# Attention scores of a hybrid encoder in unsplit float32, two heads at a time on the halves of the array's rows

## The chip, the cores and the metric

The kernel runs on one core of a Trainium2 chip. A core has a matrix engine (TensorE, PE in the profile; PEld are its weight loads), a vector engine (VectorE, DVE), a scalar engine (ScalarE, ACT), GpSimd (POOL), and SyncE (SP), which here only issues transfers. Each engine works through its own queue in order, and semaphores tie the queues together. The metric is the device time of one execution in microseconds: before the change, the median of three runs is 2033.01 us (2028.2 to 2036.88).

## The reference

Two encoder layers over 1024 tokens of width 1024, in float32. The part of a layer that matters here, with 8 query heads, 2 key/value heads and 4 memory heads of 64 dimensions:

```python
h = _rmsnorm(x, g_pre_mix[l])
zf, zq, zk, zv, zm = jnp.split(h @ w_in[l], splits, axis=-1)
q = _rope(zq.reshape(b, s, 8, 64), positions)
k = _rope(zk.reshape(b, s, 2, 64), positions)
v = zv.reshape(b, s, 2, 64)
# window attention: block of 128 queries against its own and the two neighbouring blocks of keys
scores = jnp.einsum('bnqhgd,bnjhd->bnhgqj', qb, kb) * 64 ** -0.5
probs = softmax(concat([where(valid, scores, NEG_INF), sink]))[..., :-1]
y_a = jnp.einsum('bnhgqj,bnjhd->bnqhgd', probs, vb)
# memory attention: every token against 256 memory rows
km, vm = jnp.split(_rmsnorm(mem, g_mem[l]) @ w_mem_kv[l], 2, axis=-1)
scores = jnp.einsum('bshd,bmhd->bhsm', zm, km) * 64 ** -0.5
y_m = jnp.einsum('bhsm,bmhd->bshd', softmax(scores), vm)
x = x + _rmsnorm(concat(rms(y_f), rms(y_a), rms(y_m)) @ w_out[l], g_post_mix[l])
```

`y_f` is a Fourier mixing of `zf`. A gated feed-forward network (FFN) of inner width 2816 follows, with its own norms.

## The kernel before

Tokens are handled in 8 tiles of 128. To multiply in float32 accuracy, the kernel mostly splits a value into a high part of type `float32r` (a rounded copy, made by ACT) and a low part (the rest, made by DVE or POOL), and adds three products hi*hi, hi*lo, lo*hi in PSUM (`Acc`, line 187). Such a product goes through the array once. A few products take plain `float32` operands: transposes, norms' sums, and the values of attention in part.

A layer runs these stages, each woven from two or three streams of units (`weave`): projection to k, v and z (`kvz`, tile kvp) with the Fourier products (yfp); projection to q (`q`, tile qp) with the memory attention; the window attention of key head 0 (`att_units(0)`) with the output product of the Fourier and memory groups (tile mo); the window attention of key head 1 (`att_units(1)`) with the output product of the window group and the norms (hTp); then the FFN.

A head has 64 dimensions, the array 128 rows. Before the change the kernel fills both halves of the rows with one head: for q and z the upper or lower half holds the high part and the other half the low part (`q_stacks`: ACT casts line 435, DVE subtractions line 438). The keys hold, in two arrays, the high part twice and the low part twice (`dup_stacks`: ACT lines 424 and 425, DVE lines 428 and 429). So a score tile is two products on the whole array, q's stack by the high keys and by the low keys, line 788 for window scores (tile sc, 384 columns, or 256 at the two ends) and line 901 for memory scores (tile ms, 256 columns). DVE adds the mask and takes the row maximum (line 789) or the maximum alone (line 903), ACT takes the exponential (lines 801 and 906), POOL divides by the sum (lines 812 and 912). PE transposes the probabilities (tile pT line 825, mpT line 922), and the values' product follows.

For key head 0 (`g == 0`) the transposed probabilities are split (ACT line 176, DVE line 177), and v stands as high and low part side by side, so that line 840 (tile av) runs two products of 512 columns on the whole array; `fold` adds the two halves of the outcome (ACT line 861, DVE line 863). For key head 1 and for the memory the probabilities are copied in float32 by ACT (lines 830 and 924), and two products go to the two halves of the array's *columns*, one head or pair of heads on each (av line 833, mav line 932).

PSUM has two buffers each under the tags sc, pT, av and pd; score tiles take sc. A scheduler of the framework fixes each engine's order of instructions ahead of the run by its own estimate of times, so the order isn't that of the program's text: products whose operands or buffer it deems late are moved behind others.

On-chip memory is handed out by hand in numbered slots of 256 float32 per partition (`at`), in an area of float32r, an area of float32, and separate tiles (`TURNED`, `reflex`, `turned`) which can change type; a separate tile is taken anew once all readers of its earlier content are done.

Of the kernel before, what the change touches and what calls it, by code (L numbers as in the profile page):

```python
# [11 lines left out]
F32 = mybir.dt.float32  # L12
# [7 lines left out]
P = 128  # L20
D = 1024
S = 1024
# [17 lines left out]
TURNED = {32: 8, 56: 8, 112: 8, 120: 4}  # L40
# [29 lines left out]
def tile_encoder(ctx: ExitStack, tc: tile.TileContext, T, C, out):  # L70
# [89 lines left out]
    mps, phs, yys = Ring(56, 58, 32, 34), run(16, 3, 4), run(104, 2, 4)  # L160
# [259 lines left out]
    def dup_stacks(dsts, src):  # L420

        for j, (kh, kl) in enumerate(dsts):
            r, o = slice(64 * j, 64 * j + 64), slice(64 - 64 * j, 128 - 64 * j)
            nc.scalar.copy(kh[r], src[r])
            nc.scalar.copy(kh[o], src[r])
        for j, (kh, kl) in enumerate(dsts):
            r, o = slice(64 * j, 64 * j + 64), slice(64 - 64 * j, 128 - 64 * j)
            nc.vector.tensor_tensor(out=kl[r], in0=src[r], in1=f32(kh[r]), op=ALU.subtract)
            nc.vector.tensor_tensor(out=kl[o], in0=src[r], in1=f32(kh[r]), op=ALU.subtract)

    def q_stacks(dsts, src):

        for j, dst in enumerate(dsts):
            r = slice(64 * j, 64 * j + 64)
            nc.scalar.copy(dst[r], src[r])
        for j, dst in enumerate(dsts):
            r, o = slice(64 * j, 64 * j + 64), slice(64 - 64 * j, 128 - 64 * j)
            nc.vector.tensor_tensor(out=dst[o], in0=src[r], in1=f32(dst[r]), op=ALU.subtract)


    class Memory:
# [62 lines left out]
        def load(self):  # L504
            raw = at(32, 2, NMEM)
            nc.sync.dma_start(raw, kvd[self.l, :, 0:512].rearrange("p (i c) -> p i c", i=2))
            self.v = at(6, 2, 4, HD)
            nc.sync.dma_start(self.v, kvd[self.l, :, 512:1024].rearrange("p (t h d) -> p t h d", t=2, h=4))
            km = shaped(reflex(F32R), (2, 2, 2, NMEM))
            self.km = [km[:, i] for i in range(2)]  # L510
            for ci in range(2):
                dup_stacks([(self.km[ci][:, j, 0], self.km[ci][:, j, 1]) for j in range(2)], raw[:, ci])


    class Mix:
# [193 lines left out]
        def kvz_load(self):  # L709

            self.wkvz = load_w512(self.win, FW + AW, self.g)
            self.vst, self.zst, self.kvr = {}, {}, {}

        def kvz(self, t):
            half, c = divmod(t, 4)
            if c == 0:
                self.vst[half] = at(96 + 4 * half, 4, 2, 2, HD, dt=F32R)
                z = at(104 + 8 * half, 2, 2, 512, dt=F32R)
# [848 lines left out]
```

## Time and profile before

| | |
|---|---|
| median of three runs | 2033.01 us |
| lowest, highest | 2028.2, 2036.88 us |
| profiled execution's own time | 2032.38 us |
| span of its instructions | 2030.4 us |
| mean granted TensorE clock | 0.994 of full speed |

The profile page shows the busy time of each engine, then the costliest groups of instructions, each with line, engine, operation, written and read tiles, count, busy time, mean duration in ns, and the idle time before it with the work that ended it. The chain of waits follows the work that ended last back from the end, step by step. The profile names a float32r operand in a PE row f32 as well; what tells them apart is the line. A plain float32 product leaves two records for each product, and so does its weight load. "128\*64" in a PE row is a product that uses half the array's columns.

The layer's stages lie at about 85 to 140 us (kvz and Fourier), 140 to 200 (q and memory), 200 to 290 (window attention, key head 0) and 290 to 372 (key head 1) in layer 0, and about 1070 to 1380 in layer 1.

### The profile page before, as it was taken

What the parts mean: (1) busy time and instruction counts of PE and PEld (TensorE: products, weight loads), DVE (VectorE), ACT (ScalarE), POOL (GpSimd) and SP (SyncE); (2) the same over time, 40 slices, a digit from 0 to 9 for tenths busy, and PEclk for the clock granted to TensorE, in tenths of its full rate; (3) what the DMA queues carried; (4) which work ended last, traced back from release to release, by engine and by line L of the source; (5) the groups of instructions that cost most, each with busy time, mean ns of one, the idle gap of its engine ahead of it and who ended that gap; (6) DMA issues with size and microseconds to landing.
All of it is one profiled execution on the core that took longest, in us unless ns stands there. A gap on an engine that the chain in (4) does not pass through costs nothing.

```text
span 2030.4 us, 28325 instructions
## 1 busy us (share of the span) xinstructions
PE 1984.7 (98%) x9587; PEld 1631.2 (80%) x9587; DVE 1492.6 (74%) x2346; ACT 1049.7 (52%) x2204; POOL 684.9 (34%) x811
## 2 busy tenths in 40 slices
PE   8999999999999999999999999999999999999998
PEld 7877878778888888887888778877788888887886
DVE  5566767897877776778876668679786776778766
ACT  6476877643333333554555768686333333346441
POOL 4344445224334333002423644451433433410011
PEclk9999999999999999999999999999999999999999
DMA  6110333434333324879831113244333323269973
GB/s 213 62 58 22 109 104 115 146 109 130 104 109 100 103 88 139 297 266 324 286 142 54 54 58 115 85 144 135 106 118 114 116 82 114 96 209 354 314 265 125
DMA packets 181889, 288.56 MB, mean 142 GB/s; under 512 B 15560, under 2 KB 81648, under 8 KB 181744
## 3 DMA queue, kind: packets, MB, share of 16 engines
q1 hardware_dynamic: 173680, 267.88, 39.7%
q10 hardware_dynamic: 8064, 18.88, 2.4%
q8 instruction: 75, 1.23, 0.2%
q14 instruction: 70, 0.57, 0.1%
HBM read 220.11 MB, written 66.58 MB: 141 GB/s over the span
## 4 chain that ended last, share of the span: by engine, by line
PE 86%; DVE 5%; DMA 3%; ACT 2%; issue 2%; POOL 1%; SPq 0%; DVEq 0%; POOLq 0%; ACTq 0%
PE fo L1330 17%; PE qc L1181 11%; PE qx L1181 11%; PE qy L1181 11%; PE mo L187 8%; PE qz L1181 5%; PE kvp L187 4%; PE qp L187 3%; PE zT L187 2%; PE sc L788 2%; PE pT L825 2%; PE av L833 1%; PE qa L1181 1%; PE mav L932 1%; PE av L840 1%
## 5 line engine op out<-in xcount | busy, mean ns | idle before, releaser
L1330 PE MATMUL fo<-arena_r 128*128 128x512 f32 x1512 | 354.2, 391 | 6.0 <-ACT big L1355 3.8
L1330 PEld LDWEIGHTS fo<-arena_r 128*128 128x128 f32 x1512 | 283.6, 188 | 65.6 <-ACT big L1355 4.6
L176 ACT CAST arena_r<-arena_f 128x512 fp32r<-128x512 f32 (+2 forms) x344 | 185.9, 571 | 179.5 <-DMA arena_f<-actd 66.6
L1181 PE MATMUL qc<-arena_r,flex 128*128 128x512 f32 x912 | 220.2, 390 | 0.0
L177 DVE TENSOR_TENSOR arena_r<-arena_f,arena_r 128x512 fp32r<-128x512 f32 x262 | 182.0, 727 | 46.9 <-ACT arena_r L176 39.0
L1171 ACT CAST flex<-arena_f 128x512 fp32r<-128x512 f32 x148 | 91.9, 621 | 235.0 <-PE qy L1181 73.3
L1181 PEld LDWEIGHTS qc<-arena_r,flex 128*128 128x128 f32 x912 | 171.2, 188 | 37.0
L1181 PE MATMUL qy<-arena_r,flex 128*128 128x512 f32 x576 | 139.9, 390 | 2.3 <-ACT flex L1171 2.3
L1171 ACT CAST arena_r<-arena_f 128x512 fp32r<-128x512 f32 x92 | 57.1, 621 | 159.1 <-DVE arena_f L1168 63.6
L1172 DVE TENSOR_TENSOR flex<-arena_f,flex 128x512 fp32r<-128x512 f32 x148 | 110.9, 750 | 28.4 <-ACT flex L1171 28.2
L1181 PEld LDWEIGHTS qy<-arena_r,flex 128*128 128x128 f32 x576 | 107.9, 188 | 25.3 <-ACT flex L1171 2.7
L1215 POOL TENSOR_TENSOR arena_f<-arena_f 128x512 f32<-128x512 f32 x36 | 47.3, 1315 | 237.5 <-ACT arena_f L1186 237.5
L1181 PE MATMUL qx<-arena_r 128*128 128x512 f32 x360 | 119.5, 389 | 0.0
L1181 PE MATMUL qy<-arena_r 128*128 128x512 f32 x480 | 116.7, 390 | 0.0
L1172 DVE TENSOR_TENSOR arena_r<-arena_f,arena_r 128x512 fp32r<-128x512 f32 x92 | 68.2, 742 | 63.2 <-ACT arena_r L1171 62.8
L1181 PE MATMUL qz<-arena_r,flex 128*128 128x512 f32 x320 | 106.8, 395 | 0.0
L1181 PEld LDWEIGHTS qy<-arena_r 128*128 128x128 f32 x480 | 90.3, 188 | 18.9 <-ACT arena_r L1171 0.2
L1168 DVE TENSOR_TENSOR arena_f<-arena_f 128x512 f32<-128x512 f32 x90 | 98.1, 1098 | 5.5 <-DMA arena_f<-in_w_ffn_in 3.9
L1222 POOL TENSOR_TENSOR arena_f<-arena_f 128x512 f32<-128x512 f32 x36 | 60.0, 1667 | 120.2 <-DVE arena_f L1221 120.2
L187 PE MATMUL mo<-big,arena_r 128*128 128x512 f32 x384 | 100.2, 399 | 0.3 <-ACT arena_f L1031 0.2
L1181 PE MATMUL qx<-flex,flex 128*128 128x512 f32 x304 | 100.1, 390 | 0.0
L1242 POOL TENSOR_TENSOR arena_f<-arena_f,flex 128x512 f32<-128x512 f32 x32 | 51.8, 1619 | 139.5 <-ACT flex L1233 83.7
(315 smaller groups left out, 4659.8 us busy)
## 6 DMA issues: line engine op xcount, KB each, us to landing
arena_f<-in_w_ffn_out SPq DMA_DIRECT2D x264, 256.0 KB, 4.7
actd<-arena_f SPq DMA_DIRECT2D x154, 256.0 KB, 2.5
arena_f<-actd SPq DMA_DIRECT2D x154, 256.0 KB, 4.4
arena_f<-in_w_ffn_in SPq DMA_DIRECT2D x46, 512.0 KB, 3.7
big<-in_w_ffn_in SPq DMA_DIRECT2D x40, 512.0 KB, 4.5
arena_f<-in_w_in SPq DMA_DIRECT2D x40, 256.0 KB, 2.9
arena_f<-in_x SPq DMA_DIRECT2D x16, 512.0 KB, 4.3
arena_f<-in_w_out SPq DMA_DIRECT2D x32, 256.0 KB, 2.7
```

Source lines behind the costliest of these rows:

```text
L176: nc.scalar.copy(hi, src)
L177: return (lo_eng or nc.vector).tensor_tensor(out=lo, in0=src, in1=f32(hi), op=ALU.subtract)
L187: mm(self.dst, a, b, start=self.i == 0, stop=self.i == self.n - 1)
L788: mm(pt, lhs, self.kst[g][i][:, k0 * P : k1 * P], start=i == 0, stop=i == 1)
L1168: nc.vector.tensor_tensor(out=s, in0=x, in1=y, op=op)
L1171: self.cast = nc.scalar.copy(w[:, 0], s)
L1172: nc.vector.tensor_tensor(out=w[:, 1], in0=s, in1=f32(w[:, 0]), op=ALU.subtract)
L1181: mm(pt, a, b, start=start and n == 0, stop=n == 11, skip_group_check=not start)
L1215: G(out=self.u2, in0=self.u2, in1=self.p1, op=ALU.add)
L1222: G(out=self.p5, in0=self.p1, in1=self.p5, op=ALU.add)
L1242: (G if i % 2 else V).tensor_tensor(out=a[i], in0=c, in1=g[i], op=ALU.mult)
L1330: mm(pt, ab[:, 0, x, sl], ab[:, 1, y], start=new and first and j == 0, stop=last and j == 2, skip_group_check=not new)
```

## The change

q, z and the keys stay plain float32 and are not split. A pair of heads lies on the two halves of the rows: the even head's 64 dimensions on rows 0 to 63, the odd head's on rows 64 to 127, as the transposes leave them; keys of a window key head are copied to both halves, memory keys are as loaded. Each head's score tile is now one float32 product of 64 rows by 128 columns of the array, and the two heads of a pair write two PSUM buffers. The memory attention goes by pairs of heads and half as many tokens at a time. The values of key head 0 are done as those of key head 1 were; every other copy of transposed probabilities there is DVE's. `dup_stacks`, `q_stacks`, `fold` and `values_32` go. More slots become separate tiles, and two operands of the FFN and one ring change places.

```diff
-TURNED = {32: 8, 56: 8, 112: 8, 120: 4}
+TURNED = {16: 8, 32: 8, 56: 8, 64: 8, 72: 8, 80: 8, 96: 8, 104: 8, 112: 8, 120: 4}
...
-    mps, phs, yys = Ring(56, 58, 32, 34), run(16, 3, 4), run(104, 2, 4)
+    mps, yys = Ring(56, 58, 34, 14), run(88, 2, 4)
...
         def load(self):
-            raw = at(32, 2, NMEM)
-            nc.sync.dma_start(raw, kvd[self.l, :, 0:512].rearrange("p (i c) -> p i c", i=2))
+            self.k = at(32, 2, NMEM)
+            nc.sync.dma_start(self.k, kvd[self.l, :, 0:512].rearrange("p (i c) -> p i c", i=2))
...
-            km = shaped(reflex(F32R), (2, 2, 2, NMEM))
-            self.km = [km[:, i] for i in range(2)]
-            for ci in range(2):
-                dup_stacks([(self.km[ci][:, j, 0], self.km[ci][:, j, 1]) for j in range(2)], raw[:, ci])
...
-            split(vst[:, :, 0, :], vst[:, :, 1, :], r[:, P : 2 * P].rearrange("p (g d) -> p g d", g=2), nc.gpsimd)
+            nc.gpsimd.tensor_copy(self.v32[:, :, t, :], r[:, P : 2 * P].rearrange("p (g d) -> p g d", g=2))
...
-            q_stacks([self.zst[half][j][:, :, c * P : c * P + P] for j in range(2)], zt)
+            nc.scalar.copy(self.zf[:, half, :, c * P : c * P + P], zt)
...
-                dup_stacks([(self.kst[g][0][:, sl], self.kst[g][1][:, sl]) for g in range(2)], ktf)
+                for g, copy in enumerate((nc.scalar.copy, nc.vector.tensor_copy)):
+                    for o in range(2):
+                        copy(self.kf[64 * o : 64 * o + 64, g, sl], ktf[64 * g : 64 * g + 64])
...
-            q_stacks([self.qst[half][j][:, :, c * P : c * P + P] for j in range(2)], qt)
+            nc.scalar.copy(self.qf[half][:, :, c * P : c * P + P], qt)
...
-            for h in range(4):
-                pt = ps([W], "sc", "sc")
-                lhs = self.qst[half][h % 2][:, 2 * g + h // 2, c * P : c * P + P]
-                for i in range(2):
-                    mm(pt, lhs, self.kst[g][i][:, k0 * P : k1 * P], start=i == 0, stop=i == 1)
-                nc.vector.tensor_tensor_reduce(
-                    out=es_[h // 2][:, h % 2, :W], in0=pt, in1=mask[:, m0 : m0 + W], op0=ALU.add, op1=ALU.max,
-                    scale=1.0, scalar=-3e38, accum_out=rmax[:, h : h + 1],
-                )
+            for hp in range(2):
+                pts = [ps([W], "sc", "sc") for _ in range(2)]
+                for s in range(2):
+                    r = slice(64 * s, 64 * s + 64)
+                    mm(pts[s], self.qf[half][r, 2 * g + hp, c * P : c * P + P], self.kf[r, g, k0 * P : k1 * P], start=True, stop=True)
+                for s in range(2):
+                    nc.vector.tensor_tensor_reduce(
+                        out=es_[hp][:, s, :W], in0=pts[s], in1=mask[:, m0 : m0 + W], op0=ALU.add, op1=ALU.max,
+                        scale=1.0, scalar=-3e38, accum_out=rmax[:, 2 * hp + s : 2 * hp + s + 1],
+                    )
...
-                pp = phs(2, 512, dt=F32R)
-                ph, pl = pp[:, 0], pp[:, 1]
-                split(ph, pl, pT.rearrange("p h q -> p (h q)"))
-                lhs = self.vst[(k0 + j) // 4][:, (k0 + j) % 4, g].rearrange("p a d -> p (a d)")
-                for i, p_ in enumerate((ph, pl)):
-                    mm(av, lhs, p_, start=j == 0 and i == 0, stop=j == nk - 1 and i == 1)
...
+                (nc.vector.tensor_copy if (self.pfi % 2 and not g) else nc.scalar.copy)(pf, pT.rearrange("p (k s) q -> p s k q", s=2))
+                for s in range(2):
+                    rhs = pf[:, s].rearrange("p k q -> p (k q)")
+                    mm(av[64 * s : 64 * s + 64, 0 : 2 * P], self.v32[:, g, k0 + j], rhs, start=j == 0, stop=j == nk - 1)
+            nc.scalar.copy(dst, av[:, 0 : 2 * P].rearrange("p (k q) -> p k q", k=2))
+
+        def att_begin(self, g):
+
+            pf = turned((16, 112)[g], 4, 2, 2, P)
+            self.pfs, self.pfi = [pf[:, i] for i in range(4)], 0
             if g:
...
+                v = at(4, NT, HD)
+                nc.gpsimd.tensor_copy(v, self.v32[:, 1])
+                self.v32 = v[:, None].to_broadcast([P, 2, NT, HD])
+                reflex(F32R, 16)
+                reflex(F32R, 96)
...
-        def mem_scores(self, h, half):
+        def mem_scores(self, half, pr, b):
...
+            pts = [ps([2, NMEM], "ms", "sc") for _ in range(2)]
+            for j in range(2):
+                c = 2 * b + j
+                for s in range(2):
+                    r = slice(64 * s, 64 * s + 64)
+                    mm(pts[s][:, j], self.zf[r, half, pr, c * P : c * P + P], self.mem.k[r, pr], start=True, stop=True)
...
-    HB = {1: (64, 72), 2: (80, 88), 5: (16, 24), 6: (96, None), 3: (0, 8), 7: (32, 40), 4: (104, None)}
+    HB = {1: (64, 104), 2: (80, 72), 5: (16, 24), 6: (96, None), 3: (0, 8), 7: (32, 40), 4: (88, None)}
...
+            if i == 5:
+                reflex(F32R, 64)
+                reflex(F32R, 104)
             if 5 <= i < 9:
                 hb.plain(0, i - 5)
...
-                reflex(F32R, 112)
+                for k in (72, 80, 112):
+                    reflex(F32R, k)
```

The orders that the scheduler makes are shown at three places of layer 0; a row has the line, the operation, the tile written and the tiles read, the shape, and xN where N in a row are alike. The number behind a tile's name tells one use of it from another. After the change, line 762 holds the window scores, 855 the memory scores, 800 and 875 the transposes of probabilities, 806 and 885 the values' products.

PE in the window attention of key head 0, third block and after, before the change: each sc tile's two products stand together.

```order
L788 MATMUL sc_2281<-arena_r 128x384 x2
L788 MATMUL sc_2338<-arena_r 128x384 x2
L187 MATMUL mo_2134<-big_2036,arena_r 128x512 x3
L187 MATMUL mo_2134<-big_2037,arena_r 128x512 x3
L825 MATMUL pT_2246<-const,arena_f 128x128
L825 MATMUL pT_2255<-const,arena_f 128x128
L788 MATMUL sc_2342<-arena_r 128x384 x2
```

PE in the same attention, near its end, with the change; sc_2636 and sc_2637 are the two heads of one pair, sc_2642 begins the next.

```order
L762 MATMUL sc_2636<-flex_838,flex_1781 128x384
L806 MATMUL av_2504<-flex_2031,flex_836 64x256 x2
L940 MATMUL ssp_2599<-const,arena_f 128x2
L806 MATMUL av_2504<-flex_2031,flex_836 64x256 x4
L940 MATMUL ssp_2599<-const,arena_f 128x2
L762 MATMUL sc_2637<-flex_838,flex_1781 128x384
L762 MATMUL sc_2642<-flex_838,flex_1781 128x384
```

A pair's second product stands behind other work here, beside the next pair's first. Over both layers 22 of the 64 pairs stand together, and 9 second products stand directly ahead of the next pair's first.

PE in the memory attention, woven with the projection to q (qp, qT), before the change: four products for each ms tile.

```order
L771 MATMUL qT_1748<-const,arena_f 128x128 x3
L901 MATMUL ms_1676<-flex_1429,arena_r 128x256 x4
L901 MATMUL ms_1684<-flex_1429,arena_r 128x256 x4
L771 MATMUL qT_1748<-const,arena_f 128x128
L922 MATMUL mpT_1704<-const,arena_f 128x128 x4
L932 MATMUL mav_1698<-arena_f 64x512 x2
```

And with the change, where ms_1556 takes the upper rows and ms_1557 the lower ones:

```order
L745 MATMUL qT_1548<-const,arena_f 128x128 x4
L855 MATMUL ms_1556<-arena_f,flex_837 128x256
L855 MATMUL ms_1557<-arena_f,flex_837 128x256
L855 MATMUL ms_1556<-arena_f,flex_837 128x256
L855 MATMUL ms_1557<-arena_f,flex_837 128x256
L875 MATMUL mpT_1580<-const,arena_f 128x128 x4
```

In 12 of 16 units of both layers the four products stand so; elsewhere they are torn, or two of the same half stand side by side.

DVE between the last keys and the first memory scores, before the change; big is a part of q's weights, zT and kT are transposed z and keys, flex_1429 holds the memory's keys.

```order
L407 SCALAR_TENSOR_TENSOR big_1343<-arena_f,const,big_1343 128x512
L428 TENSOR_TENSOR arena_r<-kT_1165,arena_r 64x512
L429 TENSOR_TENSOR arena_r<-kT_1165,arena_r 64x512
L428 TENSOR_TENSOR arena_r<-kT_1165,arena_r 64x512
L429 TENSOR_TENSOR arena_r<-kT_1165,arena_r 64x512
L438 TENSOR_TENSOR flex_92<-zT_1369,flex_92 64x2x128 x2
L701 TENSOR_TENSOR arena_f<-qp_1389,ct_1417 128x512
L703 TENSOR_TENSOR arena_f<-qp_1389,st_1421 128x512
L428 TENSOR_TENSOR flex_1429<-arena_f,flex_1429 64x256
```

And with the change:

```order
L407 SCALAR_TENSOR_TENSOR big_1337<-arena_f,const,big_1337 128x512
L718 COPY flex_838<-kT_1167 64x512 x2
L857 TENSOR_REDUCE nmx_1419<-ms_1424 128x2
L857 TENSOR_REDUCE nmx_1419<-ms_1425 128x2
L676 TENSOR_TENSOR arena_f<-qp_1376,ct_1404 128x512
L678 TENSOR_TENSOR arena_f<-qp_1376,st_1408 128x512
```

The subtractions for keys, z and memory keys are gone from DVE's queue; two copies of keys are left.

More of the change, by code (lines that the diff above doesn't have):

```diff
@@ L772, in q_turn @@
             if c == 0:
-                self.qst[half] = [at((64, 0)[half] + 8 * i, 4, 512, dt=F32R) for i in range(2)]
-            q_stacks([self.qst[half][j][:, :, c * P : c * P + P] for j in range(2)], qt)
+                self.qf[half] = turned((64, 72)[half], 4, 512)
+            nc.scalar.copy(self.qf[half][:, :, c * P : c * P + P], qt)
         def att_scores(self, g, n):
@@ L825, in att_values @@
                     nc.tensor.transpose(pT[:, h, :], es_[h // 2][:, h % 2, j * P : j * P + P], ident)
-                if g:
-                    pf = self.pfs[self.pfi % 4]
-                    self.pfi += 1
-                    nc.scalar.copy(pf, pT.rearrange("p (k s) q -> p s k q", s=2))
-                    for s in range(2):
-                        rhs = pf[:, s].rearrange("p k q -> p (k q)")
-                        mm(av[64 * s : 64 * s + 64, 0 : 2 * P], self.v32[:, k0 + j], rhs, start=j == 0, stop=j == nk - 1)
-                    continue
@@ L846, in values_32 @@
-        def values_32(self):
-            self.v32 = at(4, NT, HD)
-            for half in range(2):
-                v = self.vst[half][:, :, 1]
-                nc.gpsimd.tensor_tensor(out=self.v32[:, 4 * half : 4 * half + 4], in0=f32(v[:, :, 0]), in1=f32(v[:, :, 1]), op=ALU.add)
-            pf = turned(112, 4, 2, 2, P)
-            self.pfs, self.pfi = [pf[:, i] for i in range(4)], 0
-        def fold(self, av, dst):
-            cut = lambda ap: ap.rearrange("p (h s q) -> p s h q", s=2, q=P)
-            avh, avl = cut(av[0:64]), cut(av[64:128])
-            d = [dst[64 * s : 64 * s + 64] for s in range(2)]
-            for s in range(2):
-                nc.scalar.copy(d[s], avl[:, s])
-            for s in range(2):
-                nc.vector.tensor_tensor(out=d[s], in0=avh[:, s], in1=d[s], op=ALU.add)
+                pf = self.pfs[self.pfi % 4]
@@ L910, in mem_scores @@
             nc.vector.reciprocal(rden, den)
-            for b in range(4):
-                nc.gpsimd.tensor_scalar(
-                    out=e[b // 2][:, b % 2], in0=e[b // 2][:, b % 2], scalar1=rden[:, b : b + 1], scalar2=1.0, op0=ALU.mult, op1=ALU.mult
-                )
+            for i in range(4):
+                ei = e[i // 2][:, i % 2]
+                nc.gpsimd.tensor_scalar(out=ei, in0=ei, scalar1=rden[:, i : i + 1], scalar2=1.0, op0=ALU.mult, op1=ALU.mult)
             return e
@@ L1440, in tile_encoder @@
             r.i = 0
-        mix.values_32()
+        mix.att_begin(1)
         att = mix.att_units(1)
```

77 lines of the change are left out of this document (24 added, 53 removed).

## The prediction

> **What bounds the kernel now.** I read the page first: the busy shares and the chain that ended last.
>
> ```profile
> span 2030.4 us, 28325 instructions
> PE 1984.7 (98%) x9587; PEld 1631.2 (80%) x9587; DVE 1492.6 (74%) x2346; ACT 1049.7 (52%) x2204; POOL 684.9 (34%) x811
> PE 86%; DVE 5%; DMA 3%; ACT 2%; issue 2%; POOL 1%; SPq 0%; DVEq 0%; POOLq 0%; ACTq 0%
> ```
>
> TensorE (PE) makes up 86% of the chain, but that is an average over the whole program. The change touches only the stretch of each layer from the key/value/z projection to the end of the attentions, so I asked for busy times there (columns: stretch, its length, then busy time of PE, PEld, DVE, ACT, POOL).
>
> ```profile
> 85.00:140.00 55.00, 53.73 (x278) 44.75 (x276) 34.47 (x71) 38.05 (x93) 26.54 (x43) 1.00 0.22 65
> 140.00:200.00 60.00, 59.17 (x308) 45.52 (x308) 39.63 (x67) 35.06 (x97) 29.29 (x51) 0.97 0.04 12
> 200.00:290.00 90.00, 87.52 (x472) 72.61 (x469) 69.33 (x201) 71.44 (x192) 38.96 (x64) 1.00 0.35 116
> 290.00:372.00 82.00, 81.71 (x490) 64.03 (x488) 53.91 (x118) 60.57 (x154) 42.64 (x72) 1.00 0.33 115
> ...
> sum 597.00, PE 588.06 PEld 473.14 DVE 418.67 ACT 422.61 POOL 286.60; mean PE 65.34 PEld 52.57 DVE 46.52 ACT 46.96 POOL 31.84
> ```
>
> The sum is over both layers: of 597.0 us, PE lacks work in 8.9 us only. DVE is idle for 178 us and ACT for 174 us there. So taking work off DVE and ACT can give back at most those 8.9 us and what follows from them; everything else is decided by whether PE's own instructions get longer or shorter. PE's busy time overstates its streaming, since the records overlap, so I price PE by the chain of waits, where a piece lasts from the end of the work before it to its own end (columns: start, length, what).
>
> ```profile
> 141.45 6.41 PE qp L187 x21
> ...
> 162.54 1.00 PE mav L932 x2
> 163.54 1.81 PE qp L187 x7
> ...
> 168.29 1.01 PE mav L932 x4
> ...
> 183.72 1.86 PE mav L932 x6
> ...
> 215.48 1.38 PE mo L187 x6
> ...
> 226.93 0.70 PE sc L788 x4
> ...
> 253.46 0.46 PE av L840 x2
> 253.91 0.44 PE pT L825 x4
> ...
> 263.58 0.48 PE sc L788 x4
> ...
> 293.89 0.58 PE av L833 x4
> ...
> 295.76 1.35 PE pT L825 x11
> ```
>
> **The unit prices.** A split product on the whole array costs 0.70 / 4 = 0.175 us at 384 columns (sc) and 0.48 / 4 = 0.12 us at 256 columns; at 512 columns it is 1.38 / 6 = 0.23 us (mo, av L840).
>
> An unsplit float32 product on part of the array exists today only on column halves (av L833, mav L932):
>
> ```profile
> L788 PE MATMUL sc<-arena_r 128*128 128x384 f32 x192 | 49.0, 355 | 0.1
> L840 PE MATMUL av<-arena_r 128*128 128x512 f32 x88 | 31.0, 420 | 2.2 <-DVE flex L863 2.0 <-DVE arena_r L177 0.2
> L833 PE MATMUL av<-flex,arena_f 128*64 128x256 f32 x176 | 26.3, 398 | 0.0
> L932 PE MATMUL mav<-arena_f 128*64 128x512 f32 x64 | 23.4, 612 | 0.0
> L788 PE MATMUL sc<-arena_r 128*128 128x256 f32 x64 | 12.7, 298 | 0.5 <-ACT arena_f L906 0.3 <-DVE rmax L789 0.2
> L901 PE MATMUL ms<-flex,arena_r 128*128 128x256 f32 x64 | 10.4, 289 | 2.1 <-ACT flex L425 1.3 <-DVE flex L438 0.8
> L901 PE MATMUL ms<-flex,flex 128*128 128x256 f32 x64 | 10.2, 286 | 0.0
> ```
>
> The code issues 88 av and 32 mav products; the rows count 176 and 64, so each float32 product is two passes. In the chain one lone mav product of 512 columns (x2) takes 1.00 us and a pair on the two halves (x4) 1.01: the halves run at the same time, and a product without its partner costs as much as a pair. A pair of 256 columns takes 0.58, so 256 columns cost 1.01 - 0.58 = 0.43 us for both passes, with 0.15 us to enter. Three products in a row (x6), which need two steps, check it: 0.15 + 2 x 0.86 = 1.87 against 1.86. Leaving costs too: seven qp right behind mav take 1.81 instead of 7 x 0.23 = 1.61, eleven transposes behind av 1.35 instead of 11 x 0.11 = 1.21; I take 0.17. So a visit to half-array products costs 0.32 us plus 0.43 us for each step of 256 columns or 0.65 of 384: **0.75** (one step of 256), **0.97** (one of 384), **1.18** (two of 256), **1.61** (three), **2.04** (four). Those are column halves. The change's scores are on row halves, which no row shows; I take the same prices, the nearest rows being the only partial-array ones, and vary them below.
>
> The Trainium skill, "TensorEngine Tiling (Array Packing)", Key Properties, says that changing the tiling mode drains TensorE, whichever way it is tiled. That speaks against this change, and the 0.15 and 0.17 us agree for column halves; by it the sum is the one below, and if rows were exempt it would be the first rival's.
>
> **The change on PE.** How often PE enters the half-array form follows from its order of instructions, counted over both layers.
>
> - *Window scores.* 128 products, 96 of 384 and 32 of 256 columns. Only 22 of 64 pairs stand together; with 9 accidental neighbours of opposite halves there are 97 visits of one step: 75 of 384 and 22 of 256. 75 x 0.97 + 22 x 0.75 = 89.3 us, against 192 x 0.175 + 64 x 0.12 = 41.3. **+48.0.** Had all 64 pairs stayed whole: 48 x 0.97 + 16 x 0.75 = 58.6, so 31 of it is the tearing.
> - *Memory scores.* 64 products of 256 columns: 12 visits of two good pairs (1.18), one with both products of one half ahead of the other's (1.61), four of two products on the same half (1.18), three of one step (0.75): 22.8 us, against 128 x 0.12 = 15.4. **+7.4.**
> - *Memory values.* 12 visits of two pairs and 8 of one, at 256 columns: 20.2. Before: 11 visits of two 256-column steps (1.18), six of four (2.04): 25.2. **-5.0.**
> - *Window values.* The first group of heads leaves 88 split products of 0.23 (20.2 us) for 88 float32 ones on column halves, as the second group has them. Visits before: 23 of one step, 9 of two, 1 of three = 29.5; after: 38, 18, 5 = 57.8. 57.8 - 29.5 - 20.2 = **+8.1.**
>
> PE gets 48.0 + 7.4 - 5.0 + 8.1 = **58.5 us** more.
>
> **The change on DVE and ACT** costs nothing on the path, and frees much.
>
> ```profile
> L177 DVE TENSOR_TENSOR arena_r<-pT,arena_r 128x512 fp32r<-128x512 f32 x44 | 29.4, 687 | 1.3 <-ACT arena_r L176 0.8
> L438 DVE TENSOR_TENSOR arena_r<-qT,arena_r 64x512 fp32r<-64x512 f32 x32 | 22.0, 689 | 9.9 <-ACT arena_r L435 9.4
> L863 DVE TENSOR_TENSOR flex<-av,flex 64x256 f32<-64x256 f32 x32 | 13.2, 413 | 1.0 <-ACT flex L861 0.7
> ```
>
> DVE loses the 22.0 and 13.2 us whole, and of the 44 subtractions on pT 22 stay as copies of at most 0.69 us (-14.3): about 50 us, and more with the z and key stacks. ACT's casts fall with them. PE pays back the waits that these caused: 2.1 (ms) and 2.2 (av L840) in the rows above, and two more:
>
> ```profile
> L187 PE MATMUL qp<-big,arena_r 128*128 128x512 f32 x288 | 81.5, 404 | 1.7 <-DVE big L407 1.7
> L988 PE MATMUL ssp<-const,arena_f 128*128 128x2 f32 x192 | 26.2, 240 | 1.1 <-DVE arena_r L438 1.1
> ```
>
> The 1.7 is a weight's low part queued on DVE behind the four key subtractions. After the wait at 141 us the 21 qp take 6.41 instead of 21 x 0.23 = 4.83 us, at a granted clock of 0.97 in that stretch: 1.6 more. Relief in all 2.1 + 2.2 + 1.7 + 1.1 + 1.6 = **8.7 us**. It could be nothing, if z's turn is then the late one, and no more than 8.9 + 1.6 = 10.5. The new areas add waits before they are written again (q's first half before the FFN's operands, at the sixth unit); their last readers, the scores of the first four blocks, are issued two units earlier, so I cost this at zero. The copy of v moves from ACT to POOL, busy 286.6 of 597.0 us; no transfer is added or moved.
>
> **Sum.** 2032.4 (this execution's time; span 2030.4, median of the runs 2033.0) + 58.5 - 8.7 = **2082 us**.
>
> **Rivals.**
> 1. *Row halves cost no entry and exit.* The 117 visits of scores lose 0.32 us each, 37.4: **2045**. For it: all 128 columns keep draining the same way as with the full array. Against: the only partial form in the trace pays at both ends.
> 2. *Row halves do not run together.* Then 31 window visits have a second step (25 x 0.65 + 6 x 0.43 = 18.8) and 12 memory visits two more, two others one (26 x 0.43 = 11.2): **2112**. For it: both halves write the same 128 output partitions, which column halves do not. Against: they write different tiles. The Trainium skill, "TensorE: Matmul & The Clock Gate", Part 3, gives 3.07 times for four row tiles, so it expects them to overlap; no run shows it yet.
> 3. *Faster: a product over 64 rows takes one pass and no entry cost.* Scores then cost 75 x 0.325 + 22 x 0.215 = 29.1 (-12.2), memory scores 38 steps of 0.215 = 8.2 (-7.2); with +8.1, -5.0 and -8.7 that is 25.0 us less: **2007**. It decides once PE's gain on scores exceeds the 8.1 us of the values. Against it: half the columns did not save a pass on av.
> 4. *The pairs come out whole on the chip,* so that the change does what it says: 2082 - 31 = 2051. The engine takes products in its queue's order, so I give it little.
>
> **How the numbers follow.** Forecast 0.56, rival 1 0.15, rival 2 0.18, rival 3 0.06, rival 4 0.05. The range 2043 to 2114 reaches from rival 1 to rival 2. A measurement of this kernel tells about 0.5% (10 us) from no change: slower by that takes the forecast, rivals 2 and 4 and two thirds of rival 1, 0.89; same the rest of rival 1, 0.05; faster rival 3, 0.06.
>
> **What would show it.** Sc rows of half the height at two records for each product; lone ones of 384 columns at 0.8 us in the chain, a pair no longer than that; transposes behind them late by 0.15 us; PE's busy still 98% with the added 50 us all between 85 and 430 us and again in the second layer; the L425, L438 and L863 waits gone. I am wrong if a lone score product takes under 0.5 us, or if the FFN's stretches change by more than 5 us.

## The result, and the profile after

The changed kernel takes 2089.87 us (median of five runs, 2086.92 to 2096.43) against 2032.72 us of the kernel before on the same chip: 1.0289 times as long, with an interval of 1.0271 to 1.0307. The forecast was 2082, in a range of 2043 to 2114. The profiled execution is the longest of the five, so a second profile was taken later (run `e9_after_again`, below), and the comparison by stages uses that one.

The page of the changed kernel, its first lines and the chain of waits by engine:

```profile
span 2094.6 us, 28238 instructions
PE 2042.9 (98%) x9739; PEld 1612.0 (77%) x9739; DVE 1419.3 (68%) x2212; ACT 1002.7 (48%) x2094; POOL 688.9 (33%) x809
PE 83%; DVE 5%; DMA 5%; issue 3%; ACT 2%; POOL 2%; SPq 0%; DVEq 0%; POOLq 0%; ACTq 0%
```

DVE lost 73 us of work and ACT 47, and PE gained 58 us: the change took work from engines that had time and gave work to the one that sets the end. The busy times by stretch of layer 0 (columns as in the prediction) show that most waits it could win back there are gone, and that this buys little:

```profile
85.00:140.00 55.00, 55.00 (x282) 45.14 (x281) 27.46 (x55) 33.06 (x78) 30.64 (x44) 1.00 0.22 65
140.00:200.00 60.00, 60.00 (x348) 45.92 (x346) 26.43 (x49) 29.39 (x88) 28.69 (x50) 1.00 0.08 23
200.00:290.00 90.00, 89.42 (x450) 55.89 (x448) 47.00 (x147) 51.27 (x140) 35.94 (x57) 0.98 0.29 95
290.00:400.00 110.00, 109.34 (x553) 70.28 (x552) 64.21 (x141) 70.53 (x180) 45.97 (x79) 1.00 0.29 100
```

From 85 to 200 us PE lacks nothing now; before it lacked 2.1 us there. The groups of instructions by form show the new products, on 64 rows of the array and with two records for each product:

```profile
L762 PE MATMUL sc<-flex,flex 64*128 64x384 f32 x192 | 69.6, 542 | 0.0
L762 PE MATMUL sc<-flex,flex 64*128 64x256 f32 x64 | 18.1, 428 | 0.4 <-DVE rmax L764 0.4
L855 PE MATMUL ms<-arena_f,flex 64*128 64x256 f32 x128 | 21.4, 404 | 0.0
L885 PE MATMUL mav<-arena_f 128*64 128x256 f32 x96 | 14.3, 398 | 0.0
```

96 + 32 window products leave 192 + 64 records, so a float32 product over half the rows takes two passes, as one over half the columns did. The chain of waits prices them (start, length, what):

```profile
134.61 0.63 PE ms L855 x2
...
137.65 0.63 PE ms L855 x4
...
149.27 1.06 PE ms L855 x8
...
207.72 0.84 PE sc L762 x2
...
220.00 1.59 PE mo L187 x6
221.71 1.39 PE mo L187 x6
...
236.79 0.85 PE sc L762 x4
```

A lone score product of 384 columns (x2) takes 0.84 us and a pair (x4) 0.85; at 256 columns both take 0.63. The two row halves run at the same time, and a product without its partner costs what the pair costs. Two pairs in a row take 1.06, so the second step is 0.43, the price that column halves had. What is left of the first step, 0.63 - 0.43 = 0.20, is the entry, not 0.15. Six output products straight behind a visit take 1.59 us instead of 1.38 or 1.39: leaving costs 0.2.

**Where the time went.** The table gives, for each layer, the start of the last memory value product and of the last mo product, the first transpose of q in layer 1 and the last product of the FFN, in the profile before and in the second profile after. Of the second, the rows that carry it (first and last start stand behind the durations; the layers were asked for apart):

```profile
L885 PE MATMUL mav<-flex,arena_f x16: 379/379/430, 159.0 to 207.9; 128*64 128x256 f32 x16
L187 PE MATMUL mo<-flex,arena_r x96: 387/393/505, 303.9 to 403.2; 128*128 128x512 f32 x96
L745 PE MATMUL qT<-const,arena_f x32: 270/272/329, 1173.8 to 1232.9; 128*128 128x128 f32 x32
L885 PE MATMUL mav<-flex,arena_f x16: 379/379/430, 1190.9 to 1238.8; 128*64 128x256 f32 x16
L187 PE MATMUL mo<-flex,arena_r x96: 387/393/499, 1341.0 to 1430.7; 128*128 128x512 f32 x96
L1282 PE MATMUL fo<-flex x1176: 387/389/632, 832.6 to 2077.9; 128*128 128x512 f32 x196
```

and of before:

```profile
L932 PE MATMUL mav<-arena_f x32: 592/592/643, 162.5 to 211.0; 128*64 128x512 f32 x32
L187 PE MATMUL mo<-flex,arena_r x96: 387/393/774, 292.0 to 381.8; 128*128 128x512 f32 x96
L771 PE MATMUL qT<-const,arena_f x32: 270/272/275, 1145.5 to 1202.2; 128*128 128x128 f32 x32
L932 PE MATMUL mav<-arena_f x32: 592/593/644, 1161.3 to 1209.5; 128*64 128x512 f32 x32
L187 PE MATMUL mo<-flex,arena_r x96: 387/393/500, 1292.6 to 1376.6; 128*128 128x512 f32 x96
L1330 PE MATMUL fo<-arena_r x1512: 387/389/628, 807.7 to 2021.3; 128*128 128x512 f32 x189
```

| stretch ends at | before | after | grows by | forecast, both layers |
|---|---|---|---|---|
| memory, layer 0 | 211.0 | 207.9 | -3.1 | |
| window, layer 0 | 381.8 | 403.2 | +24.5 | |
| FFN 0, up to q of layer 1 | 1145.5 | 1173.8 | +6.9 | |
| memory, layer 1 | 1209.5 | 1238.8 | +1.0 | -4.1 (with layer 0; measured -2.1) |
| window, layer 1 | 1376.6 | 1430.7 | +24.8 | +53.9 (with layer 0; measured +49.3) |
| FFN 1 | 2021.3 | 2077.9 | +2.5 | 0 (with FFN 0; measured +9.4) |

The forecast's terms are sorted so: memory +7.4 - 5.0 and the relief of 2.1, 1.7, 1.1 and 1.6; window +48.0 + 8.1 and the relief of 2.2. One of them belongs to another row: the wait of 1.7 us ended at 1137 us, ahead of the first transpose of q in layer 1, so in the row FFN 0. There another wait has come in its place. From the waits of PE between kvp and qT of layer 1, before and in the second profile after (us in total, times, the longest):

```profile
PE qp L187 <- DVE big L407: 1.7, 1, 1.7
```

```profile
PE kT L712 <- POOL arena_f L681: 1.8, 1, 1.8
```

Before, kT waited for POOL there for 0.3 us. With the 1.7 in its row, the forecast for memory is -2.4 and for the FFN -1.7.

### The profile page after: what moved, and what is told of

It reads as the page before. It is cut to its first block, busy times and chain, and to the rows that moved or that the text cites. A ratio compares the mean times of both kernels' runs of the same rounds, so it can differ in the third digit from the quotient of the medians.

```text
span 2094.6 us, 28238 instructions
## 1 busy us (share of the span) xinstructions
PE 2042.9 (98%) x9739; PEld 1612.0 (77%) x9739; DVE 1419.3 (68%) x2212; ACT 1002.7 (48%) x2094; POOL 688.9 (33%) x809
## 4 chain that ended last, share of the span: by engine, by line
PE 83%; DVE 5%; DMA 5%; issue 3%; ACT 2%; POOL 2%; SPq 0%; DVEq 0%; POOLq 0%; ACTq 0%
PE fo L1282 14%; PE qc L1133 10%; PE qy L1133 10%; PE qx L1133 10%; PE mo L187 9%; PE qz L1133 5%; PE qp L187 4%; PE sc L762 4%; PE kvp L187 3%; PE av L806 2%; DMA arena_f<-actd 2%; PE zT L187 2%; PE pT L800 2%; DMA arena_f<-in_w_ffn_out 2%; PE ssp L940 1%
## 5 line engine op out<-in xcount | busy, mean ns | idle before, releaser
L1282 PE MATMUL fo<-flex 128*128 128x512 f32 x1176 | 282.8, 393 | 8.6 <-ACT big L1307 4.8
L1282 PEld LDWEIGHTS fo<-flex 128*128 128x128 f32 x1176 | 222.6, 190 | 55.9 <-ACT big L1307 5.2
L1133 PE MATMUL qc<-flex,flex 128*128 128x512 f32 x912 | 220.2, 390 | 0.0
L176 ACT CAST flex<-arena_f 128x512 fp32r<-128x512 f32 (+1 forms) x228 | 130.5, 606 | 144.9 <-DMA arena_f<-actd 64.6
L1133 PEld LDWEIGHTS qc<-flex,flex 128*128 128x128 f32 x912 | 171.2, 188 | 36.9
L177 DVE TENSOR_TENSOR flex<-arena_f,flex 128x512 fp32r<-128x512 f32 x204 | 146.2, 741 | 65.4 <-ACT flex L176 55.4
L1282 PE MATMUL fo<-arena_r 128*128 128x512 f32 x672 | 165.9, 392 | 6.2 <-ACT big L1307 6.2
L1282 PEld LDWEIGHTS fo<-arena_r 128*128 128x128 f32 x672 | 126.8, 189 | 32.9 <-ACT big L1307 6.6
L1124 DVE TENSOR_TENSOR flex<-arena_f,flex 128x512 fp32r<-128x512 f32 x148 | 111.4, 755 | 26.4 <-ACT flex L1123 26.4
L1133 PE MATMUL qx<-flex,arena_r 128*128 128x512 f32 x384 | 125.7, 389 | 0.0
L1124 DVE TENSOR_TENSOR arena_r<-arena_f,arena_r 128x512 fp32r<-128x512 f32 x92 | 69.5, 756 | 63.7 <-ACT arena_r L1123 63.4
```

The lines of the kernel that those rows point to most:

```text
L176: nc.scalar.copy(hi, src)
L177: return (lo_eng or nc.vector).tensor_tensor(out=lo, in0=src, in1=f32(hi), op=ALU.subtract)
L1124: nc.vector.tensor_tensor(out=w[:, 1], in0=s, in1=f32(w[:, 0]), op=ALU.subtract)
L1133: mm(pt, a, b, start=start and n == 0, stop=n == 11, skip_group_check=not start)
L1282: mm(pt, ab[:, 0, x, sl], ab[:, 1, y], start=new and first and j == 0, stop=last and j == 2, skip_group_check=not new)
```

## The experiments

**1 and 2. Is it the tearing of the pairs?** The scheduler of the changed kernel leaves 97 visits to the row halves for 128 window products. In the first kernel a pair's products wait for the maximum of the pair before, and so stay together (69 visits); in the second they are issued in the wrong order for their buffers, and nearly every pair is torn (119 visits).

```diff
 # e1_whole_pairs
+                with tc.high_priority():
+                    for s in range(2):
...
+                        m = mm(pts[s], ...)
+                        if s == 0 and scl[0] is not None:
+                            tc.add_manual_dep(m.ins, scl[0].ins.name, ..., reason="whole pairs")
 # e2_torn_pairs
-                for s in range(2):
...
-                    mm(pts[s], ...)
+                with tc.high_priority():
+                    first = None
+                    for s in (1, 0):
...
+                        with tc.issue_after(first.ins) if first is not None else ExitStack():
+                            first = mm(pts[s], ...)
```

> The change as it is, except that a window pair's first product also waits for the vector engine's last maximum of the pair before it, and both get a higher priority, so that in PE's order 59 of 64 pairs stand together (22 before) and the scores make 69 visits to the row halves instead of 97. Theory (the added time is PE's: each visit costs entry, steps and exit, and a lone product costs a full step): by the changed kernel's own chain a visit of 384 columns is 0.84 + 0.17 us, of 256 columns 0.63 + 0.17; 51 x 1.01 + 18 x 0.80 = 65.9 us against 75 x 1.01 + 22 x 0.80 = 93.4; the values' visits are torn a little more (+4.9). 2089.9 - 27.5 + 4.9 = 2067 us. Rival (the time sits in new waits and lower clock that the tearing has nothing to do with): 2085 to 2095. Rival (the extra wait on the vector engine costs what the whole pairs bring): 2090 or more.

> The change as it is, except that a pair's second product is issued ahead of its first, which tears nearly all pairs in PE's order: 1 of 64 stands together, and there are 119 visits for scores instead of 97 (92 of 384 columns, 27 of 256). Theory: 92 x 1.01 + 27 x 0.80 = 114.5 us against 93.4, so +21.1, and the values' visits are torn more as well, +9.1: 2120 us. Rival (waits and clock, not the tearing): 2085 to 2100.

Measured: 2058.72 us (ratio 1.0122, 1.0106 to 1.0138) with whole pairs, 2109.21 (1.0364, 1.0347 to 1.0382) with torn ones. The time goes with the number of visits: 28 fewer visits for scores than in the changed kernel save 31.2 us, 22 more cost 19.3. The expected 22.6 and 30.2, which hold the values' visits too (61 in the changed kernel, 71 and 80 here), are 9 and 11 us off. Reckoned afterwards, two things close this. A visit that another half-array product follows at once pays no exit (the section on the prediction has the numbers); counted in the traces, this holds for 28 of the window's visits in the changed kernel and for 39 and 56 here, so that 11 x 0.17 = 1.9 us more are saved and 28 x 0.17 = 4.8 us less are paid. And the clock differs. Added up from 80 us to the last product, (1 - granted clock) x length, called the clock's loss from here on, is 11.9 us in the changed kernel's second profile, 5.1 with whole pairs and 6.8 with torn ones. The sums are then -22.6 - 1.9 - 6.8 = -31.3 and 30.2 - 4.8 - 5.1 = 20.3.

So the visits move the time as priced, and the tearing is shown to be some 24 of the whole loss of 57 us; the other 6.8 of the 31.2 are clock, which nothing ties to the tearing (the most torn kernel loses hardly more). Whole pairs still do not reach the kernel before.

**3 to 6. The parts by themselves.** Into the kernel before went the memory attention of the change alone, or this and the values of key head 0. In the first two kernels z got slots that operands of mo take next (a wait of mo for their casts was then seen in the trace, 4.2 us in the third kernel); in the other two z stands in slot 112:

```diff
 # e3, e4
-TURNED = {32: 8, 56: 8, 112: 8, 120: 4}
+TURNED = {32: 8, 56: 8, 104: 8, 112: 8, 120: 4}
+                    self.zf = turned(104, 2, 2, 512)
 # e5, e6
+                    self.zf = turned(112, 2, 2, 512)
 # all four: mem_scores by pairs of heads
...
-                        mm(pt[:, j], lhs, self.mem.km[h // 2][:, h % 2, i], start=i == 0, stop=i == 1)
+                    mm(pts[s][:, j], self.zf[r, half, pr, c * P : c * P + P], self.mem.k[r, pr], start=True, stop=True)
 # e4 and e6: att_values as in the change
```

> The memory attention alone as in the change (z and memory keys unsplit, heads of a pair on the row halves, half as many tokens at a time); window scores and all window values as before. Theory: memory scores about +6.6 us on PE, memory values -5.7, the waits at 138 to 141 us in layer 0 (2.1) and the slow stretch behind them (1.6) gone: 2032.7 - 2.8 = 2030 us, within 0.3% of the kernel before. Rival (the row halves cost wherever they are used): 2040 or more.

> As the memory attention alone, and the values of key head 0 unsplit on the column halves too; only the window scores stay split on the whole array as before. Theory: the values cost PE +8.3 us and give back the 2.2 us of waits for the fold, so 2030 + 6 = 2036 us; the changed kernel minus this one, about 54 us, is then the window scores' share. Rival (the values and their copies carry a good part of the loss): 2050 or more.

> Memory attention alone as in the change, once more, with one slot moved: in e3 z stood where the split operands of the output product are put next, and those waited until the last scores had read z. Its trace shows that as PE waiting for the scalar engine's cast of them, 1.6 us at 196 us and 2.6 us at 1203 us, and a stretch of 3.4 us at half clock behind the second (1.7 us lost). Here z stands in slot 112 and the operands keep 104. Theory: e3's excess over the kernel before is this wait, so 2039.6 - 1.6 - 2.6 - 1.7 = 2033.7 us, the same as before within 0.2%. Rival (the row halves themselves cost the 6 us): 2038 to 2041.

> Memory attention and the values of key head 0 as in the change, window scores as before, with the same slot moved. Theory: the wait in e4 was 1.8 us in each layer, so 2044.4 - 3.6 = 2040.8 us, some 7 us over e5 for the values (8.3 on PE less 2.2 of waits); the changed kernel minus this one, 49 us, is the share of the window scores (predicted 48.0). Rival (no effect of the slot): 2044.

Measured: memory alone 2039.6 us (1.0029, 1.0017 to 1.0041) and 2039.4 (1.0035, 1.0019 to 1.0051); with the values 2044.43 (1.0047, 1.0027 to 1.0067) and 2045.15 (1.0072, 1.0049 to 1.0094). The theories of all four were too low, and the rivals of the last two (2038 to 2041, and 2044) came true. The slot explains nothing: the wait of mo is gone with the other slot, but the kernel is no faster. So the memory part by itself costs 6 to 7 us where its terms make -4.1; the values of key head 0 cost 5 to 6 more, where 8.1 - 2.2 = 5.9 was expected; and what is left for the window scores is 2089.9 - 2045.2 = 44.7, against 48.0.

At its end in layer 1 the memory part of the fifth kernel loses time to waits and to the clock (busy time of PE and granted clock, then DMA):

```profile
1200.00:1207.00 7.00, 6.52 (x38) 1.00 0.38 123
1207.00:1214.00 7.00, 5.77 (x25) 0.74 0.49 153
1214.00:1221.00 7.00, 7.00 (x26) 0.53 0.10 38
```

PE waits for 1.7 us between 1200 and 1214 and then runs at a lower clock: (1 - 0.74) x 7 + (1 - 0.53) x 7 = 5.1 us are lost to the clock. Before, the same place (1201 to 1222 us) has a clock of 1.00. But the clock's loss from 80 us on is 6.8, 5.1, 6.8 and 6.8 us in runs 3 to 6 and 6.8 before: the low clock stands at another place, and there is no more of it. So it does not explain the 6 to 7 us. Of the waits, 2.1 us in the whole run are new ones of the transposes on POOL, which divides the probabilities:

```profile
PE mpT L916 <- POOL arena_f L908: 2.1, 5, 0.6
```

**7. What if a product took one pass?** q and the window keys are read as float32r without being split. This leaves out their low parts in the window scores, so the time is that of a kernel that computes less.

```diff
-                    self.kf = turned(80, 2, S)
+                    self.kf = shaped(reflex(F32R, 80), (2, S))
-                self.qf[half] = turned((64, 72)[half], 4, 512)
+                self.qf[half] = shaped(reflex(F32R, (64, 72)[half]), (4, 512))
```

> The change, with q and the window keys cast to float32r and not split, so that a window score is one pass over the array instead of two double ones; the low parts of q and k are left out of the scores. Pairs are torn much as in the change: 87 visits, 64 of 384 columns and 23 of 256. Theory (a visit costs 0.20 us to enter and 0.17 to leave whatever the type, the rest is columns): 0.37 + 384 / 2400 = 0.53 us and 0.48 us, 64 x 0.53 + 23 x 0.48 = 45.0 us against 93.4, and +2.5 for the values' visits: 2089.9 - 48.4 + 2.5 = 2044 us, still no faster than the split products on the whole array (41.3 us), because the visits alone are 32 us. Rival (tearing costs by the waits behind it, not by columns): 2070 or more. Rival (a one-pass product needs no entry): 2012 to 2025.

Measured: 2052.83 us (1.0104, 1.0083 to 1.0126). The second pass is worth most of 37 us (the scheduler also makes 87 visits for scores here instead of 97, and 70 for values instead of 61), yet even half the passes would not beat the kernel before. It is 9 us above what was expected, and the clock accounts for some of that:

```profile
206.00:213.00 7.00, 6.57 (x21) 0.54 0.11 40
297.00:304.00 7.00, 6.96 (x25) 0.55 0.00 0
304.00:311.00 7.00, 7.00 (x37) 0.71 0.02 5
```

These three stretches alone lose 0.46 x 7 + 0.45 x 7 + 0.29 x 7 = 8.4 us. The clock's loss is 17.1 us here and 11.9 in the changed kernel's second profile, so 5 of the 9 us are clock; the other 4 are not traced.

**8. Can the price of a visit be saved in the kernel before?** Its own float32 products stand on column halves, in 50 visits. Here only their order changes: the four products of a memory value tile go in a row, and so do all of a window block of key head 1. Nothing of the change is in it.

```diff
-            for mt in range(2):
-                for s in range(2):
-                    mm(av[64 * s : 64 * s + 64], self.mem.v[:, mt, 2 * pr + s], pfs[s][mt], start=mt == 0, stop=mt == 1)
+            last = None
+            for mt in (1, 0):
+                for s in (1, 0):
+                    with tc.issue_after(last.ins) if last is not None else ExitStack():
+                        last = mm(av[64 * s : 64 * s + 64], self.mem.v[:, mt, 2 * pr + s], pfs[s][mt], start=mt == 1, stop=mt == 0)
```

> The kernel before the change, with nothing unsplit; only the order of the products on the column halves is other: the four products of a memory values tile, and the four or six of a window values tile of key head 1, are issued in a row, the one whose operand comes last first. PE's order then has 24 visits to the column halves instead of 50. Theory: 8 x 2.04 us instead of 25.2 for the memory and 12 x 1.61 + 4 x 1.18 = 24.0 instead of 29.5 for the window: 8.9 + 5.5 = 14.4 us less, 2033.0 - 14.4 = 2019 us, faster than both kernels. Rival (the delay of the first products makes their readers late): 2030 to 2045.

Measured: 2018.04 us (2014.64 to 2024.63), a ratio of 0.9935 (0.9917 to 0.9953): faster than both kernels, with 24 visits instead of 50. Its chain holds only whole visits, at the prices of the prediction (0.15 + 4 x 0.43 = 1.87 and 0.15 + 3 x 0.43 = 1.44):

```profile
165.88 1.87 PE mav L941 x8
...
177.87 1.87 PE mav L941 x8
...
294.87 1.45 PE av L840 x12
303.37 1.45 PE av L840 x12
```

**9. The changed kernel once more.**

> The changed kernel once more, for a second profile: the first was taken of the slowest of its five runs (2096.4 us against a median of 2089.9), and it holds 11.0 us of waits of the FFN's products on ACT's output casts, against 3.8 before, and about 52 us at the half clock, against 27. If both belong to that one run, then the median is again 2087 to 2093, and the new profile has under 6 us of those waits and under 40 us at the half clock. If the change causes them, the waits come to 9 us or more again, and the half clock to 45 us or more, with two windows of it at the hand-over from the memory to the window attention.

Measured: 2089.72 us (ratio 1.0288, 1.027 to 1.0306). The first theory is right on the median and wrong on the waits: those of the FFN are 8.1 us, short of the 9 of the second theory but again far above the ones of before.

```profile
PE fo L1282 <- ACT big L1307: 8.1, 2, 6.0
```

```profile
PE fo L1330 <- ACT big L1355: 3.8, 2, 2.9
```

(The second fence is before: us in total, times, the longest.) The output copies on ACT, from which PE gets its PSUM buffer back, come late. The sums of this wait fall into two groups: 11.0, 8.1, 7.5, 8.6, 9.0, 9.0 and 6.8 us in the seven profiles with unsplit window scores (after, and runs 9, 1, 2, 7, 10, 11), and 3.8, 4.3, 4.8, 2.3, 4.1 and 3.5 in the six without. So the change causes it. In the second profile's chain a copy stands behind a cast that stands behind the load of its operand:

```profile
858.17 4.37 DMA arena_f<-actd
...
863.17 0.61 ACT arena_r L176
863.78 0.48 ACT big L1306
864.26 0.50 ACT big L1307
...
864.80 20.27 PE fo L1282 x81
```

The seven profiles are also those of kernels in which operands of the FFN changed places; whether that makes the loads late was not tried.

The clock is between the two theories: about 37 us at the half clock (18.7 us lost, twice that), under the 40 of the first, yet with the two windows at the hand-over from memory to window attention that the rival named, PE being busy all along (second profile):

```profile
199.00:206.00 7.00, 6.80 (x36) 1.00 0.35 114
206.00:213.00 7.00, 7.00 (x31) 0.85 0.11 40
...
1235.00:1242.00 7.00, 6.96 (x35) 0.98 0.48 146
1242.00:1249.00 7.00, 7.00 (x17) 0.54 0.10 37
```

**10. Whole pairs and grouped values.** On top of the first experiment, the values of a window block go in a row, as in the eighth.

```diff
-                for s in range(2):
-                    mm(av[64 * s : 64 * s + 64, 0 : 2 * P], self.v32[:, g, k0 + j], rhs, ...)
+                todo.append((j, pf))
+            last = None
+            for i, (jj, pf) in enumerate(todo[::-1]):
+                for s in range(2):
+                    with tc.issue_after(last.ins) if last is not None else ExitStack():
+                        last = mm(av[64 * s : 64 * s + 64, 0 : 2 * P], self.v32[:, g, k0 + jj], rhs, ...)
```

> The kernel with whole pairs of scores (2058.7 us), in which the value products of a window block, both heads' and all its key tiles', are also issued one behind the other. By the order of instructions on PE the visits to the column halves for window values fall from 71 to 38, the visits to the row halves for scores stay near (69 and 67). Theory, that a visit costs 0.32 us to enter and leave whatever is done in it, or 0.37 with the entry of 0.20 that the changed kernel's chain shows: 33 fewer make 10.6 to 12.2 us less, 2047 (2043 to 2051). Rival, that once the score pairs are whole PE has to wait for the transposes that the grouped values need, and the gain goes into such waits: 2054 to 2062, with waits of av on the copies of pT of 5 us or more. Rival, that more than the visits is gained, since waits fall too: under 2040.

Measured: 2054.75 us (1.0112, 1.0091 to 1.0134); by the ratios that is 2 us less than in the first experiment, not told apart from nothing, while the 11 that were expected lie outside. The time is the first rival's, but not its cause: PE's waits of av on the copies come to 1.7 us, not 5. From the ends of PE's records, the time put to av falls from 51.5 to 46.4 us, which is 33 entries of 0.15. The exits were expected to fall as well. By the order in the traces fewer of them go than visits: 22 of the window's visits are followed at once by another half-array product here and 39 in the first experiment, so 18 exits, 3 us, should be gone. Not even these show in the work behind them, and why stays open. The clock takes 3.4 us more in this profile than in the first experiment's (8.5 against 5.1).

**11. The memory part undone in the changed kernel.**

```diff
-            nc.scalar.copy(self.zf[:, half, :, c * P : c * P + P], zt)
+            q_stacks([self.zst[half][j][:, :, c * P : c * P + P] for j in range(2)], zt)
 # Memory.load, mem_scores, mem_probs, mem_values, mem_units as before the change
```

> The changed kernel with its memory attention put back (z and memory keys split, scores on the whole array, values of 512 columns on column halves), window scores and values as changed, in 94 visits for scores by the order of instructions instead of 97. It weighs the memory part from the other end: put alone into the kernel before, it cost 0.35% [0.19, 0.51] of 2032 us, 7 us; in the changed kernel's own trace the memory stretches are 2.6 us shorter than before. Theory that the part costs 7 us wherever it stands: this kernel takes 2090 - 7 - 3 (three visits fewer) = 2080, ratio to before 1.024. Theory that it saves PE 2 to 4 us here, since it takes the waits of this stretch away, and that the 7 us came from the hand-over to a window attention that was unchanged there: 2090 to 2091, ratio 1.0285 to 1.029. Rival from the prediction's terms, +2.4 without its relief of 6.5, back again here: 2091 to 2093.

Measured: 2081.2 us (2072.61 to 2083.08), ratio 1.023 (1.0211 to 1.025). The first theory holds and the other two fall: the memory part costs some 6 us from this end too (8.7 less, of which 3 for the visits; by the ratios, which compare with the kernel before on the same chip, it is 12 less, give or take 5). The hand-over runs at full clock here:

```profile
197.00:204.00 7.00, 7.00 (x42) 1.00 0.45 140
204.00:211.00 7.00, 7.00 (x34) 1.00 0.18 67
...
1200.00:1207.00 7.00, 7.00 (x45) 1.00 0.44 128
1207.00:1214.00 7.00, 7.00 (x33) 1.00 0.39 131
```

The clock's loss is 5.1 us in this profile, 11.9 in the second one of the changed kernel, and 6.8 before. It is tempting to put the cost of the memory part down to the clock, and of the ten profiles with the new memory attention eight have a low clock at the hand-over, two (runs 2 and 4) have none; of the three without it, none has. But the profiles do not bear it out: runs 3 to 6 have the cost without a greater loss, the two profiles of the changed kernel differ by 3.5 us among themselves (15.4 and 11.9), and the profile of run 11 is the fastest of its five, 8.6 us below its median. What the memory part costs beyond its own products stays open.

## Why the prediction was right, point by point

- **PE sets the end, and DVE's and ACT's relief is worth little: right.** 73 and 47 us less work there did not make up for 58 us more on PE; PE's busy time stayed at 98%.
- **The scheduler tears the pairs, and each visit is paid: right.** Runs 1 and 2 move the time by the visits at their price, once exits and clock are counted. Rival 4, pairs whole on the chip, falls with the chain's lone pieces of two records.
- **The prices of row halves are those of column halves: right but for the entry.** A step costs the same 0.43 us, lone and paired products cost the same. So rival 1 (free entry and exit) and rival 2 (halves one after the other) both fall: 0.63 us for a lone 256-column product is not 0.43, and a pair takes no more. The Trainium skill had it right in both sections that the prediction named: changing the mode drains TensorE ("TensorEngine Tiling (Array Packing)", Key Properties), and row tiles overlap ("TensorE: Matmul & The Clock Gate", Part 3); the 0.20 us of entry and 0.85 against 0.84 us agree. Rival 3 falls with the two records for each product.
- **Window stretches, forecast +53.9, measured +49.3.** The kind of cost was right, its size is off in the term "window scores", with errors that partly cancel. The entry is 0.20, which adds 97 x 0.05 = 4.9. The exit was charged for every visit, but where another half-array product follows, only its entry is paid: in the traces this holds for 28 of the 158 visits after and for none of the 33 before, so there are 97 more exits, 16.5 us, where 125 x 0.17 = 21.3 had been charged. From the ends of PE's records, the work behind the visits (mo, pT and ssp) grew by 19.4 us in these stretches, of which up to 3.4 are clock (5.1 us lost at 210 and 1245 us, 1.7 at 375 before); that leaves 16.0. With the entry the forecast would be 58.8, and without the clock the stretches grew by 45.9. Of these 13 us the exits are 5, and some 2 are visits that fall into the memory stretches. Another 5 are the products before, which took more than they were priced at: from the records' ends sc took 45.0 us against 41.3, and av 47.8 against 20.2 + 29.5 - 33 x 0.17 + 2.2 = 46.3. After, they took 78.5 and 47.6, where the prices with the new entry and without exits give 77.6 and 47.4.
- **Memory, forecast -4.1, measured -2.1: right as far as it goes.** The sizes of its own products were right: from the records' ends, mav falls by 5.4 us (5.0 forecast), and the waits named are gone. Most of the 2 us is the wait of 1.7 that was sorted into the wrong stretch; the step that failed there is that its relief stays, since kT waits 1.8 us for POOL in the same stretch now. By itself the part costs more than any term says, 6 to 7 us in runs 3 and 5 and about as much in run 11. New waits were put at nothing, and these runs show some (4.2 us of mo in run 3, 2.1 of the transposes in run 5), but not 10 us of them; the rest is open.
- **The FFN unchanged, "I cost this at zero": wrong.** It grew by 9.4 us, beyond the 5 us that the prediction itself set as the mark of an error. 4.3 us are the longer wait on ACT's copies, and 3.4 are clock: stretches at 477, 866 and 1894 us lose 6.8 us, where before two at 1439 and 1842 lose 3.4. The rest is small waits. That the areas' readers finish early was argued from the window attention's side; what the moved operands do to the FFN's loads was not looked at.

The misses cancel in part: 2082 forecast, +2.0 memory, -4.6 window, +9.4 FFN make 2089, and 2089.9 was measured. That the forecast lies within 8 us owes something to this luck; the mechanism does not.

## What to carry to other kernels

A product on half the array costs an entry and an exit however little is done in it, and costs the same without its partner as with it: count the visits in the order that the scheduler really issues, not the products, and keep half-array products together (in this kernel that alone brought 0.65%). Unsplit float32 halves the number of instructions but not the passes, so on a kernel that PE bounds, two heads side by side win nothing over two split products on the whole array (here a whole pair of 384 columns took 0.85 us and its exit, the four split products 0.70). Where on-chip slots change hands, look at the stage that uses them next, even if its computation did not change; that the moved operands caused the FFN's waits here was not tried.

## What the runs showed of the hardware that was not expected

The granted clock falls to half without PE having waited. In the second profile the stretch ahead of the drop is full and at full clock:

```profile
206.40:209.80 3.40, 3.40 (x17) 1.00 0.00 0
209.80:213.20 3.40, 3.40 (x11) 0.65 0.20 77
```

Just before, the chain has only half-array visits and small products of norms (sc, mav and ssp by turns from 203.7 to 211.1 us), and the six mo products behind take 2.77 us instead of 1.38. The Trainium skill, "TensorE: Matmul & The Clock Gate", Part 1, names an idle window of about 3.4 us as what brings the half clock; here the low clock lasts 3.4 us as well, but no idle window precedes it in the profile, and here the measurement decides. What brings the low clock is not shown: run 2, with the most torn pairs, has none at this place.
